# Weight tiles of the 512-column products, moved by 8 bytes within 256

## The chip, the cores and the metric

The kernel runs on one core of a Trainium2 chip. The metric is the device time of one execution in microseconds (us), as the median of several runs. Instruction durations and distances between instructions are given in nanoseconds (ns). The engines are called as in the profile: PE is TensorE's matmul, PEld its weight load, DVE VectorE, ACT ScalarE, POOL GpSimd, SP SyncE.

## The reference

One decoder layer in float32, sequence 512, model width 1024, with everything multiplied by weights that come from HBM. Cut to its products:

```
proj = h @ w_in                      # q, k, v, pool input, gate logits
y_attn = moba_attention(q, k, v) @ w_branch_attn
y_pool = multiscale_pool(p) @ w_branch_pool
mixed = sigmoid(g0) * y_attn + sigmoid(g1) * y_pool
h = layer_norm(ALPHA * h + mixed @ w_out)
a, u = split(h @ w_ffn_in)           # 2 x 2816 columns
a = causal_dwconv(a)                 # width 3
f = (gelu(a) * u) @ w_ffn_out
h = layer_norm(ALPHA * h + f)
```

## The kernel before, in words

Each float32 operand of a large product is split into two float32r tiles: hi, a rounded copy that ACT writes (line 74), and lo, the rest, which DVE writes as source minus hi (line 75). A product tile is then three matmuls that accumulate in one PSUM bank: hi with hi, hi with lo, lo with hi (`mm3`, lines 236 to 242; the v product has its own loop at line 411). Each matmul is a pair of instructions, a weight load of the 128x128 stationary operand on PEld and a matmul on PE that streams the moving operand. The load of the next pair's stationary operand runs while the present matmul streams.

Weights come in as chunks of 128 partitions by 1024 columns. `fetch` (line 128) starts the DMA into a raw tile, splits it and puts the two tiles into a ring of five slots for each of hi and lo (`slot`, line 121); a few of `w_out`'s chunks go to a pool of their own, `ext`. `weights(i)` runs `fetch` three chunks ahead. A slot is 1088 elements wide (`SLOT = D + 64`), of which 1024 are used: 4352 bytes, 17 times 256, so that all slots of the ring begin at the same place within 256 bytes.

There are two kinds of products.

- 256-column products: the moving operand is an activation of 256 columns, the stationary one is a 128x128 block of a weight tile. These are the seven-product forms of the input projection (out tiles `sai`, `sbi`, `sci`), of the gates (`sag`, `sbg`, `scg`) and of the gated MLP's first projection (`saf`, `sbf`, `scf`), in `seven`, and the first five tiles of that projection (`fi`), which run in two halves.
- 512-column products. Here the roles differ. In the pool input (`p`), the gates (`g`), the branch projections (`br`) and the rest of `fi` the weight block is stationary and the activation of 512 columns moves. In v (`v`), the output projection (`wo`) and the MLP's second projection (`foe`, `foa`, `fob`, `fod`) the activation block is stationary and 512 columns of the weight tile move. The last tile of the second projection, `fo_cut`, is cut into pieces of 256 columns, with the weight moving too.

The pools are laid out so that, without an offset, both operands of all these products begin at the same place within 256 bytes (byte 192 in this program's allocation). `slot` has an argument `near`: with it the two tiles begin `BESIDE = 2` elements, 8 bytes, behind the slot's beginning. `fetch_seven` (line 203) passes it, and `fetch` (line 151) for the first five chunks of the MLP's first projection: so the stationary operand of all 256-column products but `fo_cut` begins 8 bytes behind the moving operand's place. All 512-column products, and `fo_cut`, have both operands at the same place.

The tile framework orders each engine's instructions by a schedule and sets the semaphores; PE runs the products one behind the other in the order v, p and the first sevens, gates with attention, branch projections, the gates' sevens, output projection, MLP first projection, MLP second projection.

Of the kernel before, what the change touches and what calls it, by code (L numbers as in the profile page):

```python
# [9 lines left out]
F32R = mybir.dt.float32r  # L10
# [4 lines left out]
P = 128  # L15
S = 512
D = 1024
# [15 lines left out]
RING = 5  # L33
SLOT = D + 64
BESIDE = 2
TMP = 7
PLAIN = (3, 2)
WARM = 6
# [12 lines left out]
def layer_kernel(ctx: ExitStack, tc: tile.TileContext, xT, x, w_v, w_c, rel_bias, invcnt, w_group,  # L51
# [18 lines left out]
    def split(hi, lo, src, copy=None):  # L70
        if copy:
            copy(hi, src)
        else:
            state["hi"] = nc.scalar.activation(hi, src, AF.Copy)  # L74
        state["lo"] = nc.vector.tensor_tensor(lo, src, hi.bitcast(F32), op=ALU.subtract)  # L75
        return state["lo"]
# [30 lines left out]
    WO0 = len(chunks)  # L107
    chunks += [w_out[k * P:(k + 1) * P, :] for k in range(KT)]
    FI0 = len(chunks)
# [6 lines left out]
    FO0 = len(chunks)  # L116
# [1 line left out]
    ready = {}  # L118


    def slot(i, n, near=False):
        o = BESIDE if near else 0
        return tuple(wp.tile([P, SLOT], F32R, tag=f"w{q}", name=f"w{q}{i}", bufs=RING)[:, o:o + n]
                     for q in ("hi", "lo"))

# [2 lines left out]
    def fetch(pool=None, early=None):  # L128
        i = state["next"]
        state["next"] = i + 1  # L130
        for q, ahead in AHEAD.items():
            while coming[q]:
                key = coming[q][0]
                n, f = key
                lead_ = EARLY.get((n, f, q), ahead)
                if not homes.get((n, q)) or at[n, f, q] > i + (lead_ if q != "A" or (n, f - 1) in pair_of else 0):
                    break
                with ExitStack() as held:
                    if (n, f, q) == ("i", 1, "X"):
                        held.enter_context(tc.issue_after(state["neg"].ins))  # L140
                    if (n, f, q) in (("i", 1, "D"), ("i", 2, "A"), ("i", 2, "X"), ("i", 2, "D")):
                        held.enter_context(tc.issue_after(state["plain"].ins))
                    if (n, f, q) == ("i", 2, "X"):
                        held.enter_context(tc.issue_after(state["sum"].ins))
                    fetch_raw(coming[q].pop(0), q)
        if isinstance(chunks[i], tuple):
            ready[i] = (fetch_fo if i >= FO0 else fetch_seven)(i, *chunks[i])
            return
        raw = wp.tile([P, D], F32, tag="wraw", name=f"wraw{i}", bufs=3)
        if pool is None:  # L150
            hi, lo = slot(i, D, FI0 <= i < FI0 + RING)
        else:
            hi = pool.tile([P, D], F32R, name=f"whi{i}")
            lo = pool.tile([P, D], F32R, name=f"wlo{i}")
        parts = 2 if early else 1
        for c in range(parts):
            sl = slice(c * (D // parts), (c + 1) * (D // parts))
            (nc.scalar if early else nc.sync).dma_start(raw[:, sl], chunks[i][:, sl])
            split(hi[:, sl], lo[:, sl], raw[:, sl])
            if c == 0 and early:  # L160
                state["w0"] = raw[:, sl]
                early()
        ready[i] = (hi, lo)
# [10 lines left out]
    def fetch_raw(key, q):  # L174
        a, u = pair_of[key]
        r = raws[key, q] = homes[key[0], q](key[1])
        if q == "A":
            nc.sync.dma_start(r, a)
        elif q == "D":
            nc.sync.dma_start(r, u[:, S:])  # L180
        elif key in SUMMED:
            state["plain"] = nc.sync.dma_start(r[:, :S], u[:, :S])
        else:
            v = r.rearrange("p (a c) -> p a c", a=2)
            (pst, pn), (est, _) = u.ap
            state["plain"] = nc.sync.dma_start(
                v, bass.AP(tensor=u.tensor, offset=u.offset, ap=[[pst, pn], [0, 2], [est, S]]))
            state["acc"] = nc.gpsimd.dma_start(  # L188
                v, bass.AP(tensor=a.tensor, offset=a.offset, ap=[[pst, pn], [u.offset + S - a.offset, 2], [est, S]]),
                accum_op=ALU.add)  # L190

    def fetch_seven(i, key, q):
        n = S if q == "D" else D
        raw = raws[key, "A" if q == "Y" else q]
        if q == "X" and key in SUMMED:
            with tc.issue_after(state["Y"].ins):
                for c, o in ((slice(S, D), raws[key, "D"]), (slice(0, S), raws[key, "A"][:, :S])):
                    nc.vector.tensor_tensor(raw[:, c], raw[:, :S], o, op=ALU.add)
        if q == "Y":

            for c, o in ((slice(0, S), raws[key, "X"][:, S:]), (slice(S, D), raw[:, :S])):
                nc.vector.tensor_tensor(raw[:, c], o, raw[:, c], op=ALU.add)
        hi, lo = slot(i, n, True)
        state[q] = split(hi, lo, raw)
        return hi, lo

# [6 lines left out]
    def fetch_fo(i, name, c):  # L213
        sl = piece(c)
        n = sl.stop - sl.start
        step = {"T3": "=B11", "B11": "+B12", "T1": "+B22", "T2": "+B21", "T4": None}
        if name in step:
            raw = tw[:, sl]
        else:
            raw = wp.tile([P, D], F32, tag="wraw", name=f"wraw{i}", bufs=3)[:, :n]  # L220
            nc.sync.dma_start(raw, half(name, sl))
        hi, lo = slot(i, n)
        split(hi, lo, raw)
        then = step.get(name)
        if then and then[0] == "+":
            nc.gpsimd.dma_start(raw, half(then[1:], sl), accum_op=ALU.add)
        elif then:
            nc.sync.dma_start(raw, half(then[1:], sl))
        return hi, lo

    def weights(i):
        while state["next"] <= min(i + LEAD, state["limit"]):
            fetch()
        return ready[i]
# [97 lines left out]
    for kt in range(KT):  # L332
        xk = xr[kt // 4][:, kt % 4, :]
        if kt == 0:
            load_x(kt, xk, slice(0, 256), nc.vector.tensor_copy)
            fetch(early=lambda: load_x(kt, xk, slice(256, 512), nc.vector.tensor_copy))
        else:
            load_x(kt, xk)
            if kt % 2 == 0:
                fetch()  # L340
# [100 lines left out]
    def pool_sum(j, b, sign=1.0, eng=None):  # L441
        eng = eng or nc.gpsimd
        w = POOL_WINDOWS[j]
        pt = pb.tile([P, PAD + S], F32, tag="tmp", name=f"pt{j}", bufs=TMP)
        nc.gpsimd.memset(pt[:, :PAD], 0.0)
        state["pt"] = nc.scalar.activation(pt[:, PAD:], b, AF.Copy, scale=sign)
        cur, sh = pt, 1
        while sh < w:
            nxt = pb.tile([P, PAD + S], F32, tag="tmp", name=f"pw{j}_{sh}", bufs=TMP)
            o = 2 * sh - 1  # L450
# [251 lines left out]
    def gate_done(f, ba, u):  # L702
        if f < KT - 1:
            for br, v, scale in ((0, ba, 1.0), (1, u, -1.0)):
                nc.scalar.activation(v, v, AF.Sigmoid, scale=scale)
                nc.vector.tensor_tensor(branch[f, br], branch[f, br], v, op=ALU.mult)
            merged(f, branch[f, 0], branch[f, 1])
        else:
            for br, v, scale in ((0, ba, 1.0), (1, u, -1.0)):
                gslot[8 * br + f] = unused.pop(0)  # L710
                nc.scalar.activation(gslot[8 * br + f], v, AF.Sigmoid, scale=scale)
# [6 lines left out]
    for f in range(GSEVEN, KT):  # L718
        if f == KT - 1:
# [3 lines left out]
              lambda ba, u, f=f: gate_done(f, ba, u), first_half if f == KT - 1 else None)  # L723
# [411 lines left out]
```

## Time and profile before

| what | value |
|---|---|
| median of 3 runs | 631.38 us (631.32 to 631.77) |
| span of the profiled execution, first to last instruction | 630.0 us |
| between the span and the median of the runs | 1.4 us |
| PE busy, share of the span | 620.1 us, 98% |
| PEld / DVE / ACT / POOL busy | 552.1 / 495.0 / 346.9 / 115.3 us |
| matmuls on PE | 3904 |
| mean granted TensorE clock | 0.995 |
| moved by DMA | 105.33 MB, 167 GB/s |

For the profiled execution the profile gives the span alone; its own time is taken as the span and the 1.4 us around it. A matmul's duration in a row (389 ns for 512 columns) is its way through the pipeline; what a stream of them costs is the distance from one start to the next, called the pitch here.

### The profile page before, as it was taken

The numbers are of one execution on the slowest core, as the hardware profiler recorded it, in microseconds if no ns is written. First come the engines' busy times: TensorE is split into PE (matmuls) and PEld (weight loads), VectorE is DVE, ScalarE is ACT, GpSimd is POOL, SyncE is SP. The second block draws the span as 40 slices with busy tenths as digits, with TensorE's granted clock in tenths as the row PEclk, the third lists the DMA queues.
The fourth block names the chain that finished last, engine by engine and source line by source line (L and its number), as shares of the span: only waits on it lengthen the run. The fifth ranks groups of instructions, "written<-read, shape, count | busy, mean of one in ns | idle before, by whom it ended". The sixth has DMA issues, their size and how long they took to land.

```text
span 630.0 us, 10173 instructions
## 1 busy us (share of the span) xinstructions
PE 620.1 (98%) x3904; PEld 552.1 (88%) x3904; DVE 495.0 (79%) x751; ACT 346.9 (55%) x517; POOL 115.3 (18%) x128
## 2 busy tenths in 40 slices
PE   9999999999999999999999999999999999999994
PEld 6899998777788998889989999999998888888884
DVE  6978787776495788399767899888889649798796
ACT  6646776654634567134545665565665345555452
POOL 0133134423142101110010101101002002123302
PEclk9999999999999999999999999999999999999997
DMA  8567647522558525805096677777539946889905
GB/s 311 172 187 188 176 119 224 135 85 67 168 127 212 129 74 161 323 12 167 5 250 164 164 206 183 202 175 193 139 107 325 267 134 133 207 194 211 257 1 133
DMA packets 38912, 105.33 MB, mean 167 GB/s; under 512 B 4288, under 2 KB 4552, under 8 KB 38608
## 3 DMA queue, kind: packets, MB, share of 16 engines
q1 hardware_dynamic: 26448, 71.11, 34.1%
q0 software_dynamic: 11840, 32.53, 26.5%
q10 hardware_dynamic: 576, 1.05, 0.5%
q8 instruction: 30, 0.49, 0.3%
q14 instruction: 18, 0.15, 0.1%
HBM read 99.41 MB, written 3.17 MB: 163 GB/s over the span
## 4 chain that ended last, share of the span: by engine, by line
PE 98%; DVE 1%; DMA 1%; DVEq 0%; issue 0%
PE fi L238 5%; PE fi L241 5%; PE fi L242 5%; PE saf L238 4%; PE saf L241 4%; PE saf L242 4%; PE v L411 3%; PE br L238 2%; PE g L238 2%; PE g L242 2%; PE g L241 2%; PE wo L241 2%; PE br L241 2%; PE wo L242 2%; PE wo L238 2%; PE br L242 2%
## 5 line engine op out<-in xcount | busy, mean ns | idle before, releaser
L74 ACT ACTIVATE whi<-wraw 128x1024 fp32r<-128x1024 f32 (+1 forms) x59 | 60.2, 1027 | 44.4 <-DMA wraw<-in_w_fo 9.4
L75 DVE TENSOR_TENSOR wlo<-wraw,whi 128x1024 fp32r<-128x1024 f32 (+1 forms) x59 | 72.3, 1233 | 15.0 <-ACT whi L74 14.7
L75 DVE TENSOR_TENSOR wlo<-araw,whi 128x1024 fp32r<-128x1024 f32 x46 | 56.0, 1227 | 11.4 <-ACT whi L74 10.7
L74 ACT ACTIVATE whi<-araw 128x1024 fp32r<-128x1024 f32 x46 | 48.1, 1057 | 19.2 <-PE saf L241 4.9
L241 PE MATMUL fi<-hT_lo,whi 128*128 128x512 f32 (+1 forms) x168 | 56.3, 336 | 0.0
L242 PE MATMUL fi<-hT_hi,wlo 128*128 128x512 f32 (+1 forms) x168 | 56.3, 336 | 0.0
L238 PE MATMUL fi<-hT_hi,whi 128*128 128x512 f32 (+1 forms) x168 | 56.1, 338 | 0.0
L188 POOL DMA_DIRECT2D xraw<-in_w_fi x14 | 16.9, 1207 | 159.1 <-DMA xraw<-in_w_fi 79.4
L74 ACT ACTIVATE whi<-tw 128x1024 fp32r<-128x1024 f32 (+1 forms) x30 | 29.4, 983 | 24.1 <-PE fi L241 10.5
L75 DVE TENSOR_TENSOR wlo<-tw,whi 128x1024 fp32r<-128x1024 f32 (+1 forms) x30 | 33.3, 1126 | 7.9 <-ACT whi L74 7.8
L242 PEld LDWEIGHTS fi<-hT_hi,wlo 128*128 128x128 f32 x168 | 31.5, 188 | 3.5
L241 PEld LDWEIGHTS fi<-hT_lo,whi 128*128 128x128 f32 x168 | 31.5, 188 | 3.3
L238 PEld LDWEIGHTS fi<-hT_hi,whi 128*128 128x128 f32 x168 | 31.3, 188 | 3.4
L549 POOL TENSOR_SCALAR pp<-pp,rs 128x128 f32<-128x128 f32 (+3 forms) x32 | 25.3, 805 | 36.6 <-DVE rs L546 26.6
L238 PE MATMUL sbf<-T_hi,whi 128*128 128x256 f32 x112 | 31.2, 279 | 0.0
L241 PE MATMUL saf<-hT_lo,whi 128*128 128x256 f32 x112 | 31.2, 278 | 0.0
L238 PE MATMUL saf<-nT_hi,whi 128*128 128x256 f32 x112 | 31.2, 278 | 0.0
L238 PE MATMUL saf<-hT_hi,whi 128*128 128x256 f32 x112 | 31.1, 278 | 0.0
L242 PE MATMUL saf<-nT_hi,wlo 128*128 128x256 f32 x112 | 31.1, 278 | 0.0
L241 PE MATMUL sbf<-T_lo,whi 128*128 128x256 f32 x112 | 31.1, 278 | 0.0
L242 PE MATMUL sbf<-T_hi,wlo 128*128 128x256 f32 x112 | 31.1, 278 | 0.0
L241 PE MATMUL saf<-nT_lo,whi 128*128 128x256 f32 x112 | 31.1, 277 | 0.0
(340 smaller groups left out, 2090.5 us busy)
## 6 DMA issues: line engine op xcount, KB each, us to landing
tw<-in_w_fo POOLq DMA_DIRECT2D x20, 512.0 KB, 8.5
wraw<-in_w_fi SPq DMA_DIRECT2D x16, 512.0 KB, 3.5
araw<-in_w_fi SPq DMA_DIRECT2D x14, 512.0 KB, 4.0
xraw<-in_w_fi SPq DMA_DIRECT2D x14, 512.0 KB, 4.4
xraw<-in_w_fi POOLq DMA_DIRECT2D x14, 512.0 KB, 6.2
wraw<-in_w_c SPq DMA_DIRECT2D x10, 512.0 KB, 3.9
tw<-in_w_fo SPq DMA_DIRECT2D x10, 512.0 KB, 6.3
wraw<-in_w_fo SPq DMA_DIRECT2D x10, 512.0 KB, 7.6
```

What stands on the lines that cost most here:

```text
L74: state["hi"] = nc.scalar.activation(hi, src, AF.Copy)
L75: state["lo"] = nc.vector.tensor_tensor(lo, src, hi.bitcast(F32), op=ALU.subtract)
L188: state["acc"] = nc.gpsimd.dma_start(v, bass.AP(tensor=a.tensor, offset=a.offset, ap=[[pst, pn], [u.offset + S - a.offset, 2], [est, S]]), ...
L238: ins = nc.tensor.matmul(out_, wh, ah, start=start, stop=False, **kw)
L241: nc.tensor.matmul(out_, wh, al, start=False, stop=False, **kw)
L242: nc.tensor.matmul(out_, wl, ah, start=False, stop=stop, **kw)
L411: nc.tensor.matmul(bs[j], xs_[j][a], (wh, wl)[b], start=kt == 0 and n == 0, stop=False)
L549: nc.gpsimd.tensor_scalar(pp[:, offs[i]:offs[i] + n], pp[:, offs[i]:offs[i] + n], rs[:, i:i + 1], 1.0, op0=ALU.mult, op1=ALU.mult)
```

## The change

All split weight tiles of the ring and of `ext` now begin 8 bytes off. Where the weight is stationary (p, g, br, the rest of `fi`, and as before the sevens) the tile begins 8 bytes behind the slot's beginning. Where the weight moves (v, the output projection, the second projection with `fo_cut`) it begins 62 elements, 248 bytes, behind it, which is 8 bytes ahead of the place within 256. In either case the stationary operand then begins 8 bytes behind the moving operand's place. The tiles of `ext` become 1088 elements wide. No instruction is added, removed or reordered in the source.

```
+MOVED = 62
...
-    def slot(i, n, near=False):
-        o = BESIDE if near else 0
+    def beside(i):
+        return MOVED if i < 4 or WO0 <= i < FI0 or i >= FO0 else BESIDE
+
+    def slot(i, n):
+        o = beside(i)
         return tuple(wp.tile([P, SLOT], F32R, tag=f"w{q}", name=f"w{q}{i}", bufs=RING)[:, o:o + n]
                      for q in ("hi", "lo"))
...
-            hi, lo = slot(i, D, FI0 <= i < FI0 + RING)
+            hi, lo = slot(i, D)
         else:
-            hi = pool.tile([P, D], F32R, name=f"whi{i}")
-            lo = pool.tile([P, D], F32R, name=f"wlo{i}")
+            hi, lo = (pool.tile([P, SLOT], F32R, name=f"w{q}{i}")[:, beside(i):beside(i) + D] for q in ("hi", "lo"))
...
-        hi, lo = slot(i, n, True)
+        hi, lo = slot(i, n)
```

Chunks 0 to 3 are v's; `WO0` to `FI0` are the output projection's, from `FO0` on the second projection's.

## Rows read from the trace of the kernel before

**Rows 1.** The page: busy time of each engine, share of the span, instructions.

```profile
PE 620.1 (98%) x3904; PEld 552.1 (88%) x3904; DVE 495.0 (79%) x751; ACT 346.9 (55%) x517; POOL 115.3 (18%) x128
```

**Rows 2.** Who PE waited for: us in total, times, longest.

```profile
PE warm_ps L326 <- DVE warm L323: 1.2, 1, 1.2
```

**Rows 3.** Matmul groups by shape, whole span: count | busy us, mean ns | idle.

```profile
L238 PE MATMUL fi<-hT_hi,whi 128*128 128x512 f32 x88 | 34.3, 389 | 0.0
...
L238 PE MATMUL g<-xT_hi,whi 128*128 128x512 f32 x64 | 25.5, 399 | 0.0
L238 PE MATMUL wo<-whi,mx_hi 128*128 128x512 f32 x64 | 25.0, 390 | 0.0
...
L238 PE MATMUL foa<-whi,sd_hi 128*128 128x512 f32 x44 | 17.1, 389 | 0.0
...
L238 PE MATMUL foe<-whi,sd_hi 128*128 128x512 f32 x33 | 12.9, 390 | 0.0
...
L238 PE MATMUL br<-zT_hi,whi 128*128 128x512 f32 x32 | 12.6, 393 | 0.0
...
L238 PE MATMUL fob<-whi,sd_hi 128*128 128x512 f32 x22 | 8.6, 389 | 0.0
...
L411 PE MATMUL v<-whi,xT_hi 128*128 128x512 f32 x27 | 8.1, 413 | 0.0
...
L238 PE MATMUL p<-xT_hi,whi 128*128 128x512 f32 x16 | 6.2, 390 | 0.0
...
L238 PE MATMUL fo_cut<-whi,sd_hi 128*128 128x256 f32 x22 | 6.2, 282 | 0.0
...
L238 PE MATMUL v<-whi,xT_hi 128*128 128x512 f32 x4 | 1.6, 389 | 0.0
```

**Rows 4.** Timeline of PE, one product of the second projection: start us, us.

```profile
531.06 0.39 PE L238 MATMUL foa<-whi,sd_hi 128*128 128x512 f32 x1
...
546.02 0.39 PE L238 MATMUL fob<-whi,sd_hi 128*128 128x512 f32 x1
```

**Rows 5.** Timeline of PE, the run of 256-column pieces at the end.

```profile
616.27 0.28 PE L238 MATMUL fo_cut<-whi,sd_hi 128*128 128x256 f32 x1
...
621.07 0.28 PE L241 MATMUL fo_cut<-wlo,sd_hi 128*128 128x256 f32 x1
```

**Rows 6.** Timeline of PE, the sevens of the MLP's first projection.

```profile
340.01 0.28 PE L242 MATMUL sbf<-T_hi,wlo 128*128 128x256 f32 x1
...
470.01 0.28 PE L242 MATMUL saf<-nT_hi,wlo 128*128 128x256 f32 x1
```

**Rows 7.** Weight loads by shape, 616.2 to 621.1 us: count | busy us, mean ns.

```profile
L238 PEld LDWEIGHTS fo_cut<-whi,sd_hi 128*128 128x128 f32 x14 | 2.7, 192 | 0.0
```

**Rows 8.** Weight loads by shape, 531.1 to 546 us.

```profile
L238 PEld LDWEIGHTS foa<-whi,sd_hi 128*128 128x128 f32 x21 | 3.9, 188 | 0.8
```

**Rows 9.** Weight loads by shape, 340 to 470 us.

```profile
L238 PEld LDWEIGHTS sbf<-T_hi,whi 128*128 128x128 f32 x110 | 20.7, 188 | 0.0
```

**Rows 10.** Matmuls running at 336.43 us, by shape.

```profile
L242 PE MATMUL fi<-hT_hi,wlo 128*128 128x512 f32 x1 | 0.4, 391 | 0.0
L241 PE MATMUL fi<-hT_lo,whi 128*128 128x512 f32 x1 | 0.4, 389 | 0.0
```

**Rows 11.** Timeline of PE, three pairs between two pieces of 256 columns.

```profile
608.66 0.40 PE L238 MATMUL foe<-whi,sd_hi 128*128 128x512 f32 x1
...
609.36 0.28 PE L238 MATMUL fo_cut<-whi,sd_hi 128*128 128x256 f32 x1
```

**Rows 12.** ACT's groups by shape, 165 to 600 us.

```profile
L74 ACT ACTIVATE whi<-wraw 128x1024 fp32r<-128x1024 f32 x37 | 38.8, 1057 | 30.9 <-DMA wraw<-in_w_fo 9.0 <-DMA wraw<-in_w_fi 4.5 <-DMA wraw<-in_w_out 4.3
L74 ACT ACTIVATE whi<-araw 128x1024 fp32r<-128x1024 f32 x36 | 37.8, 1058 | 16.4 <-PE saf L241 4.9 <-PE scf L241 3.9 <-PE br L241 1.9
```

**Rows 13.** DVE by stretch: us, busy (instructions), PE clock, DMA share, GB/s.

```profile
245.30:290.60 45.30, 34.28 (x65) 1.00 0.43 156
...
516.00:606.00 90.00, 74.58 (x83) 1.00 0.76 176
```

## The prediction

> **What bounds the kernel.** I read the page first: PE is busy for 620.1 of the 630.0 us [rows 1]. Then the waits: PE waited once, 1.2 us ahead of its first matmul, and for nothing after that [rows 2]. So the end is set by the stream of weight loads and matmuls alone, and a change that only shifts where weight tiles begin can act in one way: by the pitch, the distance from one matmul's start to the next. That is read from the timeline, as first and last row of a long stretch with the count between them. Three stretches matter:
>
> - 512 columns, both operands at the same place: from 531.06 to 546.02 us lie 66 pairs (11 blocks of the contraction, two row tiles, three matmuls), 14.96 / 66 = 226.7 ns each [rows 4].
> - 256 columns, same place: 616.27 to 621.07 us, 40 pairs, 120.0 ns each [rows 5].
> - 256 columns, stationary operand 8 bytes behind: 340.01 to 470.01 us, 1125 pairs, 115.6 ns each [rows 6].
>
> At the same place the two widths differ by 106.7 ns for 256 columns, which is one column per cycle at the 2.4 GHz level; the clock rows of two stretches of 512-column work show 1.00 granted [rows 13]. So 512 columns alone are 213.3 ns, and both widths carry the same 13.3 ns on top (226.7 - 213.3, 120.0 - 106.7). With the stationary operand 8 bytes behind, only 115.6 - 106.7 = 8.9 ns are on top. What the 8 bytes are worth in 256 columns is the difference of the two, 4.4 ns a pair.
>
> **The change, part by part.** *The 512-column pairs.* Their groups count 88 (fi), 64 (g), 64 (wo), 44 (foa; fod has as many), 33 (foe), 32 (br from zT; as many from oT), 22 (fob), 27 and 4 (v) and 16 (p) for one of the three matmuls [rows 3]: 88 + 64 + 64 + 88 + 33 + 64 + 22 + 31 + 16 = 470, times three is 1410 pairs. 696 of them (p, g, br, fi) have the weight stationary, 714 (v, wo, second projection) have it moving. No row shows a 512-column stretch with the stationary operand 8 bytes behind, so the price is bounded. Below, nothing excludes that all of the 13.3 ns goes: 1410 x 13.3 = 18.8 us. Above, the dearest pitch of settled neighbours that I find is that of three pairs between two 256-column pieces, 608.66 to 609.36 us, 233 ns each [rows 11]: 6.7 ns more than now, 9.4 us in all. Between these ends I take the value of the row that differs in just this one thing at the other width: 8.9 on top instead of 13.3. The reason is that the load lies beside the beginning of the matmul it overlaps in both widths, and that at the same place the surcharge does not depend on the width; if it is one surcharge per load, the 8 bytes should cut it alike. That is 1410 x 4.4 = 6.2 us.
>
> *The last tile, fo_cut.* 22 x 3 = 66 pairs of 256 columns go from the same place to 8 bytes off [rows 3]: 66 x 4.4 = 0.3 us. The roles are reversed there (weight moving), which the 115.6 ns row does not cover; the term is small either way.
>
> *Pairs where the relation changes today.* Between 512- and 256-column products the relation of the operands jumps now and won't afterwards. One such pair is 391 ns long where its neighbour is 389 [rows 10]. There are some twenty such borders, so a few tenths of a us at most; I leave them out of the sum.
>
> *The splits.* ACT writes a hi tile in 1057 ns where it begins at the slot's beginning (`wraw` beyond the first five fi chunks) and in 1058 ns where it begins 8 bytes on (`araw`) [rows 12], so the offset costs the splitting engines nothing. Where PE gets faster, they must follow: in the second projection DVE is busy for 74.58 of 90 us, in the output projection for 34.28 of 45.3 [rows 13]. A PE that is 2% faster shortens 90 us to 88.2, still 13 us above DVE's work. Chunks are fetched three ahead, and a chunk of the second projection lasts 12 pairs, 2.7 us. If that cover were gone, each us won would come back as a wait of PE for a lo tile; nothing in the waits says it is near.
>
> *DMA and memory.* No transfer, queue entry or wait is added or moved. The three chunks in `ext` need 1536 bytes more per partition in all; that is an allocation and no instruction.
>
> **Sum.** 6.2 + 0.3 = 6.5 us off the profiled execution: a span of 623.5 us. The median lies 1.4 us above the span, so 624.9 us.
>
> **A rule against it.** The trace says that the operands' relation within 256 bytes moves the pitch by 4.4 ns. The Trainium skill's page SBUF — State Buffer, section "Who interferes with whom", gives TensorE two independent read ports, one for the moving operand and one for the weight load, and says that PE never waits on anyone. By that rule no offset could change a pitch and the sum would be 0, against the two 256-column stretches here; as a result it is the first rival.
>
> **The rivals.** *No change: the load sets the 256-column pitch, and only there.* The load rows speak for this. In the slow 256-column stretch a load lasts 192 ns [rows 7]; 8 bytes off it lasts 188 [rows 9], and that 4 ns is just about what the pitch gained. In the 512-column product the load already lasts 188 ns [rows 8] and has 227 ns to hide in. Then the offset shortens a load that sets the pace at 256 columns and is hidden at 512; the equal 13.3 ns would be an accident. Only fo_cut gains: 631.4 - 0.3 = 631.1 us. Against it: two exactly equal surcharges at two widths ask for one cause.
>
> *Slower: 512 columns are best at the same place.* The mechanism is that the moving stream, not the load, pays for the offset, over its whole width. One pair bears it out: the last 512-column matmul of fi before a seven runs beside a load that already is 8 bytes off, and is 391 ns long instead of 389 [rows 10]; it did not get shorter. If 2 ns stay with every pair, 1410 x 2 = 2.8 us are lost: 631.4 + 2.8 = 634.2 us, and up to 640.8 us at 233 ns a pair. It decides as soon as the settled pitch is above 226.7 ns plus 0.9. Against it: a single pair at a border is not a settled stretch. The 256-column pairs behind such a border take some pairs to come down to 115.6 ns as well.
>
> *One role alone gains.* If only the 696 pairs with a stationary weight win 4.4 ns, 3.1 us come off (628.3); if only the 714 with a moving one do, about the same. This lies inside the forecast's own range and has no chance of its own.
>
> **How the numbers follow.** Forecast, faster: 0.47. No change: 0.20. Slower: 0.33. A measurement of this kernel can tell about 0.2% from no change, 1.3 us or 0.9 ns a pair, so the three signs have the same chances. The forecast's own range is 616 to 630 us, from 11 ns won per pair to 1 ns. With both signs in play the range must reach into the slower case: 619 to 636 us leaves out some 0.05 below (more than 9 ns won per pair) and some 0.09 above (more than 3.3 ns lost).
>
> **What would show it.** In the profile after: the same 66 pairs of the second projection in 14.67 us (222.2 ns) for the forecast, 14.96 us for no change, 15.1 us or more for the slower case; fo_cut at about 115.6 ns, its loads at 188 ns; the same comparison in the branch projections, where the weight is stationary, tells the roles apart; no new wait on PE. The forecast is wrong if the surcharge of a 512-column pair has another cause than that of a 256-column pair, or if the settled pitch depends on something that long streams find by themselves, which the uneven pitches at borders hint at.

## The result and the profile after

The changed kernel is slower: 637.51 us median (637.2 to 638.13, four runs) against 631.54 us (631.32 to 631.77), a ratio of 1.0092 [1.0078, 1.0107]. The forecast was 624.9 us. It missed by 12.6 us, and the result lies above the range's upper end of 636 us as well. The profiled execution has a span of 636.0 us where before had 630.0, so the profile shows the 6.0 us.

The page of the kernel after, its line of busy times:

```profile
PE 626.2 (98%) x3904; PEld 552.6 (87%) x3904; DVE 495.7 (78%) x751; ACT 346.5 (54%) x517; POOL 114.6 (18%) x128
```

The waits of PE in the kernel after:

```profile
PE warm_ps L329 <- DVE warm L326: 1.2, 1, 1.2
```

PE is busy for 6.1 us longer, with as many instructions, and waits no more than before [rows 1, 2]. PE's matmuls come in the same order in both kernels. So the time lies in the pitches, as the prediction said it must. Here are first and last row of five stretches of the kernel after, from the timeline of PE (start us, us); they are the branch projections, the output projection, the 256-column sevens of the MLP's first projection, the second projection, and the pieces of `fo_cut` at the end:

```profile
171.40 0.39 PE L244 MATMUL br<-oT_lo,whi 128*128 128x512 f32 x1
...
198.62 0.39 PE L245 MATMUL br<-zT_hi,wlo 128*128 128x512 f32 x1
...
252.24 0.39 PE L244 MATMUL wo<-wlo,mx_hi 128*128 128x512 f32 x1
...
279.66 0.39 PE L244 MATMUL wo<-wlo,mx_hi 128*128 128x512 f32 x1
...
343.32 0.28 PE L241 MATMUL sbf<-T_hi,whi 128*128 128x256 f32 x1
...
469.97 0.28 PE L244 MATMUL saf<-nT_lo,whi 128*128 128x256 f32 x1
...
535.33 0.39 PE L241 MATMUL foa<-whi,sd_hi 128*128 128x512 f32 x1
...
550.62 0.39 PE L241 MATMUL fob<-whi,sd_hi 128*128 128x512 f32 x1
...
623.70 0.28 PE L241 MATMUL fo_cut<-whi,sd_hi 128*128 128x256 f32 x1
...
626.94 0.28 PE L241 MATMUL fo_cut<-whi,sd_hi 128*128 128x256 f32 x1
```

The branch and output projections of the kernel before were not among the rows shown; the same 118 pairs of each in its timeline:

```profile
170.12 0.39 PE L241 MATMUL br<-oT_lo,whi 128*128 128x512 f32 x1
...
196.87 0.39 PE L242 MATMUL br<-zT_hi,wlo 128*128 128x512 f32 x1
...
250.26 0.39 PE L241 MATMUL wo<-wlo,mx_hi 128*128 128x512 f32 x1
...
277.01 0.39 PE L241 MATMUL wo<-wlo,mx_hi 128*128 128x512 f32 x1
```

| stretch | pairs | before, ns | after, ns |
|---|---|---|---|
| branch projections, weight stationary | 118 | 26.75 us / 118 = 226.7 | 27.22 us / 118 = 230.7 |
| output projection, weight moving | 118 | 26.75 us / 118 = 226.7 | 27.42 us / 118 = 232.4 |
| second projection, weight moving | 66 | 226.7 [rows 4] | 15.29 us / 66 = 231.7 |
| sevens, not touched | 1096 | 115.6 [rows 6] | 126.65 us / 1096 = 115.6 |
| `fo_cut`, weight moving | 27 | 120.0 [rows 5] | 3.24 us / 27 = 120.0 |

These 512-column stretches have become slower, by 4.0 ns a pair where the weight is stationary and by 5.0 to 5.7 ns where it moves. What wasn't touched stayed, and the settled run of `fo_cut` did not react at all. At these pitches 696 x 4.0 + 714 x about 5.2 is 6.5 us, against 6.0 measured. Added up over both timelines, every 512-column stage takes longer: those with a stationary weight 2.5 us in all, the output and second projections 3.0, and v 0.6, which moves by as much in runs that leave it alone. The short stretches between borders lose a little less than the long ones.

The weight loads by shape (count | busy us, mean ns | idle us), first in the same stretch of the second projection, 535.4 to 550.6 us, then in `fo_cut`, 623.7 to 626.9 us, both of the kernel after:

```profile
L244 PEld LDWEIGHTS foa<-wlo,sd_hi 128*128 128x128 f32 x22 | 4.2, 189 | 1.0
...
L241 PEld LDWEIGHTS fo_cut<-whi,sd_hi 128*128 128x128 f32 x10 | 1.9, 191 | 0.0
```

The load in the second projection lasts 189 ns where it lasted 188 before, and PEld has idle time ahead of it as before [rows 8], and the pitch grew all the same. The duration of a load therefore does not tell the pitch of the pairs.

### The profile page after: what moved, and what is told of

Same layout as the page of the kernel before. It is cut to its first block, busy times and chain, and to the rows that moved or that the text cites. A ratio compares the mean times of both kernels' runs of the same rounds, so it can differ in the third digit from the quotient of the medians.

```text
span 636.0 us, 10173 instructions
## 1 busy us (share of the span) xinstructions
PE 626.2 (98%) x3904; PEld 552.6 (87%) x3904; DVE 495.7 (78%) x751; ACT 346.5 (54%) x517; POOL 114.6 (18%) x128
## 2 busy tenths in 40 slices
DMA packets 38912, 105.33 MB, mean 166 GB/s; under 512 B 4288, under 2 KB 4552, under 8 KB 38608
## 4 chain that ended last, share of the span: by engine, by line
PE 98%; DVE 1%; DVEq 0%; issue 0%
PE fi L245 5%; PE fi L244 5%; PE fi L241 5%; PE saf L241 4%; PE saf L244 4%; PE saf L245 4%; PE v L414 3%; PE br L241 2%; PE wo L245 2%; PE wo L241 2%; PE g L241 2%; PE wo L244 2%; PE g L244 2%; PE br L245 2%; PE g L245 2%; PE br L244 2%
```

## The experiments

In the kernels named pairs, and in *enter*, the whole layer is left out: they run nothing but groups of 48 (or 60) load-and-matmul pairs on fixed tiles, so their times are those of the pairs alone. All other kernels compute the layer.

### One role each

*stat_only* moves only the 696 pairs with a stationary weight:

```
     def beside(i):
-        return MOVED if i < 4 or WO0 <= i < FI0 or i >= FO0 else BESIDE
+        return 0 if i < 4 or WO0 <= i < FI0 or i >= FO0 else BESIDE
```

> Only the 696 512-column pairs whose weight is stationary (p, g, br, the rest of fi) get the 8 bytes; v, the output and the second projection stand as before. Theory A (any pair of 512 columns whose operands are 8 bytes apart loses its even pitch of 226.7 ns and runs at about 230.6 ns, whichever operand is the weight): 696 x 3.9 = 2.7 us slower, br pitch 230.6, wo and foa pitch back at 226.7. Rival B (the loss comes from the moving operand, which begins 8 bytes off its 16-byte place when the weight moves): no change in time, br at 226.7. Rival C (something else than the pitch, such as the allocation): the time moves with no change of pitch.

Measured: 634.45 us against 632.21, ratio 1.0039 [1.0026, 1.0052]. Its timeline of PE, branch projections and second projection:

```profile
170.27 0.39 PE L244 MATMUL br<-oT_lo,whi 128*128 128x512 f32 x1
...
197.49 0.39 PE L245 MATMUL br<-zT_hi,wlo 128*128 128x512 f32 x1
...
532.86 0.39 PE L241 MATMUL foa<-whi,sd_hi 128*128 128x512 f32 x1
...
547.82 0.39 PE L241 MATMUL fob<-whi,sd_hi 128*128 128x512 f32 x1
```

27.22 / 118 = 230.7 ns where the tile was moved, 14.96 / 66 = 226.7 ns where it wasn't. The loss is 2.2 us where theory A had 2.7; rival B, no loss with a stationary weight, fell.

*mov_only* moves only the 714 pairs with a moving weight, and `fo_cut`:

```
     def beside(i):
-        return MOVED if i < 4 or WO0 <= i < FI0 or i >= FO0 else BESIDE
+        if isinstance(chunks[i], tuple) and i < FO0 or FI0 <= i < FI0 + RING:
+            return BESIDE
+        return MOVED if i < 4 or WO0 <= i < FI0 or i >= FO0 else 0
```

> Only the 714 pairs whose weight moves (v, wo, second projection) and fo_cut get the 8 bytes. Theory A: 714 x 4.7 = 3.4 us slower (the changed kernel's wo ran at 232.6 ns, the second projection at 231.6), br back at 226.7 ns; the two halves add up to the 6 us. Rival B: all of the 6 us.

Measured: 636.1 us against 632.21, ratio 1.0061 [1.0046, 1.0076]. Its timeline of PE in the second projection:

```profile
532.55 0.39 PE L243 MATMUL foa<-whi,sd_hi 128*128 128x512 f32 x1
...
547.85 0.39 PE L243 MATMUL fob<-whi,sd_hi 128*128 128x512 f32 x1
```

15.30 / 66 = 231.8 ns here, while its branch projections stay at 226.7. The halves lose 0.39 and 0.61%, together 1.00%, against 0.92% for the whole; the 3.9 us here compare with 3.4 in theory A. So both roles lose, each by its own pitch, and nothing passes from one to the other.

### The other direction

*reversed* puts the stationary operand 8 bytes ahead of the moving one in the 512-column products and `fo_cut`, and leaves the other 256-column products as they were:

```
     def beside(i):
-        return MOVED if i < 4 or WO0 <= i < FI0 or i >= FO0 else BESIDE
+        if isinstance(chunks[i], tuple) and i < FO0 or FI0 <= i < FI0 + RING:
+            return BESIDE
+        return BESIDE if i < 4 or WO0 <= i < FI0 or i >= FO0 else MOVED
```

> As the changed kernel, but in all 512-column pairs and fo_cut the stationary operand begins 8 bytes ahead of the moving one instead of behind it. Theory A as it stands has no direction: as slow as the changed kernel, about 637.5 us, pitch 230 to 232. Rival D (direction decides: a load that runs ahead of the stream collides with it, one that runs behind doesn't): faster than before, up to 1410 x 4.4 = 6 us.

Measured: 640.75 us against 632.21, ratio 1.0133 [1.0116, 1.015]. Its timeline of PE in the branch projections:

```profile
172.65 0.40 PE L246 MATMUL br<-oT_lo,whi 128*128 128x512 f32 x1
...
200.19 0.40 PE L247 MATMUL br<-zT_hi,wlo 128*128 128x512 f32 x1
```

27.54 / 118 = 233.4 ns, and 232.8 in the second projection. Ahead or behind, both lose; the direction changes only how much, and rival D fell.

### The pairs alone

*pairs* runs 48 pairs for each of 11 widths with both operands at the same place. Then it moves the stationary operand, and then the moving one, in steps of 8 bytes through 256, at 512 and at 256 columns. The core of it:

```
def run(name, n, so, mo):
    b = ps.tile([P, 512], F32, tag="ps", name=name)
    for i in range(PAIRS):    # PAIRS = 48
        k, q = divmod(i, 3)
        s = sta[q == 2][:, so + k % 8 * P:so + k % 8 * P + P]
        m = mov[q == 1][:, mo + k % 4 * 512:mo + k % 4 * 512 + n]
        tc.keep_in_program_order(nc.tensor.matmul(b[:, :n], s, m, start=i == 0, stop=i == PAIRS - 1))
    ...
```

> No layer at all: 48 pairs of weight load and matmul for each of 139 settings, nothing else running. Both operands at the same place with 128 to 512 columns; then the stationary operand at 0, 8, ... 248 bytes behind it with 512 and 256 columns; then the moving operand so. Theory A: 512 columns at the same place 226.7 ns, at 8 bytes either way about 230; 256 columns 120.0 at the same place and 115.6 with the stationary operand 8 bytes behind. If one surcharge per load is right, each width at the same place costs its columns at 2.4 GHz and 13.3 ns (272 columns 126.7, 288 columns 133.3); if pairs fall into step with something of a 13.3 ns period, 272 columns cost 133.3 as 288 do. Rival E (other engines' traffic makes the difference in the layer): flat over the offsets here.

The start of each group in its timeline of PE, first by width, then by the place of the stationary operand (`a` same place, `b` 8 bytes behind, `c` 16):

```profile
41.12 0.29 PE L40 MATMUL width<-movhi,stahi 128*128 128x288 f32 x1
...
47.44 0.31 PE L40 MATMUL width<-movhi,stahi 128*128 128x320 f32 x1
...
62.80 0.36 PE L40 MATMUL width<-movhi,stahi 128*128 128x448 f32 x1
...
72.72 0.38 PE L40 MATMUL width<-movhi,stahi 128*128 128x480 f32 x1
...
104.75 0.39 PE L40 MATMUL stat_wide_a<-movhi,stahi 128*128 128x512 f32 x1
...
115.63 0.40 PE L40 MATMUL stat_wide_b<-movhi,stahi 128*128 128x512 f32 x1
...
126.71 0.39 PE L40 MATMUL stat_wide_c<-movhi,stahi 128*128 128x512 f32 x1
...
461.02 0.28 PE L40 MATMUL stat_narrow_a<-movhi,stahi 128*128 128x256 f32 x1
...
466.78 0.28 PE L40 MATMUL stat_narrow_b<-movhi,stahi 128*128 128x256 f32 x1
...
472.34 0.28 PE L40 MATMUL stat_narrow_c<-movhi,stahi 128*128 128x256 f32 x1
```

From start to next start are 48 pairs. At 512 columns 10.88 / 48 = 226.7 ns at the same place and 11.08 / 48 = 230.8 ns 8 bytes on; at 256 columns 5.76 / 48 = 120.0 and 5.56 / 48 = 115.8. These are the pitches of the layer in all four cases, with DVE, ACT and POOL idle and about 1 GB/s on the DMA queues. So they belong to PE's own stream; no neighbour is needed.

The widths show what the prediction's step could not know. The mean granted clock of this run is 0.998. Less one column per cycle of the 2.4 GHz level, the same place carries 6.32 us / 48 - 120.0 = 11.7 ns at 288 columns and 9.92 us / 48 - 186.7 = 20.0 ns at 448, beside the 13.3 at 256 and 512. At 320 and 384 columns it is 13.3 ns again, at 272 it is 12.0, at 480 and 496 16.7. So the surcharge is not one for all widths, though four of the nine from 256 up share the 13.3 ns; no run shows why. At 192 columns the last 24 pairs still take 112.6 ns each, 32.6 above the columns.

Over the 32 places of the stationary operand, 512 columns have, over the last 24 pairs of each group (the settled pitch from here on), 226.7 ns at 0 and 120 bytes and 228.3 to 234.3 at the other 30. For the moving operand it is 226.7 at 0 and 228.9 to 236.7 elsewhere. At 256 columns the order is another: 113.3 ns at 64, 88 and 168 bytes, 115.6 at 8 bytes, up to 120.1 elsewhere. With the moving operand 248 bytes behind, which is 8 bytes ahead within 256, it is 120.0 at 256 columns, as in `fo_cut`, and 232.8 at 512, where the layer has 231.7 and 232.4. In both of these ways the stationary operand lies 8 bytes behind the moving one, and the tiles are the same; what differs is where the two lie together. So that the two roles of the weight differ in the layer needs no cause but the place.

### Is it the relation alone, and is it the load?

*pairs2* repeats this with other offsets, with both operands moved together, and with loads of 64 and 32 columns in place of 128:

```
def run(name, n, so, mo, cols=P, pairs=PAIRS):
    ...
        s = sta[q == 2][:, so + k % 6 * P:so + k % 6 * P + cols]
...
for j, o in enumerate((64, 128, 192, 256, 66, 130, 194, 258)):   # elements of 4 bytes
    run(f"period_{w_}_{LETTERS[j]}", n, o, 0)
for j, o in enumerate((2, 4, 16, 32, 48)):
    run(f"both_{w_}_{LETTERS[j]}", n, o, o)
for j, o in enumerate((0, 2, 4, 8, 16)):
    run(f"half_{w_}_{LETTERS[j]}", n, o, 0, 64)
```

> No layer: 48 pairs for each setting again. (1) The stationary operand 0 to 28 bytes behind in steps of 4. (2) 256, 512, 768, 1024 bytes behind and 8 more than each: if the relation within 256 bytes is all that counts, as at 0 and at 8 bytes (226.7 and 230.6 at 512 columns, 120.0 and 115.6 at 256). (3) Both operands moved by 8, 16, 64, 128, 192 bytes together: 226.7 and 120.0 each if only the relation counts. (4) A stationary operand of 64 and of 32 columns, so that the load reads half and a quarter: if what is on top of the columns' time comes from the load's reading beside the stream, it falls with the load's length (from 13.3 ns at the same place to about 6.7 and 3.3 at 512 columns); if it is a fixed cost of a pair, it stays. (5) 0, 8, 64, 120 bytes and back in reverse order: the same pitches whatever came before, if a stream settles by itself.

Starts of some groups in its timeline of PE, the last two at 256 columns:

```profile
200.99 0.40 PE L40 MATMUL both_wide_a<-movhi,stahi 128*128 128x512 f32 x1
...
212.12 0.39 PE L40 MATMUL both_wide_b<-movhi,stahi 128*128 128x512 f32 x1
...
223.16 0.39 PE L40 MATMUL both_wide_c<-movhi,stahi 128*128 128x512 f32 x1
...
234.05 0.39 PE L40 MATMUL both_wide_d<-movhi,stahi 128*128 128x512 f32 x1
...
255.90 0.39 PE L40 MATMUL half_wide_a<-movhi,stahi 128*64 128x512 f32 x1
...
266.94 0.39 PE L40 MATMUL half_wide_b<-movhi,stahi 128*64 128x512 f32 x1
...
575.73 0.28 PE L40 MATMUL half_narrow_a<-movhi,stahi 128*64 128x256 f32 x1
...
581.20 0.28 PE L40 MATMUL half_narrow_b<-movhi,stahi 128*64 128x256 f32 x1
```

With the stationary operand 256, 512, 768 or 1024 bytes behind, the settled pitch is 226.7 ns, like 0; 8 bytes more bring 230.5 to 230.8 each time, so at these two places the pattern of the stationary operand repeats every 256 bytes (for the moving one this was not run). But both operands moved together by 8 bytes have 11.13 / 48 = 231.9 ns, by 16 bytes 230.0, and by 64 bytes 226.9: the relation is not all, the place of both counts too. And at 512 columns a load of half the columns makes the pair no faster but slower, 11.04 / 48 = 230.0 ns at the same place; a quarter has 231.7. At 256 columns it is the other way: half has 5.47 / 48 = 114.0 ns (113.3 settled), a quarter 117.8, where the whole load has 120.0. A surcharge that the load pays by its length, once per pair, is ruled out by the 512 columns and by the quarter being dearer than the half.

Two further parts of this run: steps of 4 bytes up to 28 gave 230.0 to 235.0 ns at 512 columns and 115.6 to 133.3 at 256; and four places were run in one order and back, where each had its pitch again but 64 bytes at 256 columns, which had 117.8 ns forth and 113.3 back.

### Places that were best for 256 columns in the pairs

Can the layer have the 113.3 ns? *near64*, *near88* and *near168* leave the 512-column products at the same place, as before, and move the 256-column weights from 8 to 64, 88 and 168 bytes:

```
-BESIDE = 2
+BESIDE = 16     # near64; 22 in near88, 42 in near168
```

> The kernel before with one number changed: the stationary operand of its 2172 256-column pairs (the sevens and the first five fi tiles) begins 64 instead of 8 bytes behind the moving one; 512-column pairs stay at the same place. Theory A2 (the settled pitch of a stream of pairs is a property of its width and the operands' relation within 256 bytes, so the test of pairs alone gives the layer's): 113.3 ns a pair instead of 115.6, 2172 x 2.2 = 4.8 us faster, ratio 0.992; 512-column pairs unchanged at 226.7. Rival F (in the layer the other engines' writes and the blocks' order set the pitch, and 8 bytes were found there): pitch unlike the test's, no gain or a loss.

> The same with 88 bytes, the second place at which the test of pairs alone settled at 113.3 ns, though 80 and 96 bytes, 8 to either side, gave 118.6 and 117.2. Theory A2: 113.3 ns a pair, 4.8 us faster as with 64 bytes. Rival F: another pitch. A smooth dependence on the distance (rival G): about 116 ns or more, as its neighbours.

> The kernel before with the stationary operand of the 2172 256-column pairs 168 bytes behind the moving one, the third place at which the test of pairs settled at 113.3 ns. Theory A3 (relation and width leave a stream one or a few settled cycles, and which of them it falls into depends on how it starts): between 113.3 and 118 ns, and not the same in each stage; if 113.3 in all stages, 4.8 us faster than before. Theory A2 (the pair test's number is the only one): 113.3 everywhere.

Measured: near64 636.57 us against 631.9, ratio 1.0072 [1.006, 1.0085]; near88 628.89 against 631.9, 0.9958 [0.9944, 0.9971]; near168 638.77 against 631.88, 1.0107 [1.009, 1.0124]. The same pitch in the pairs, three answers in the layer: the sevens of near64 run at 117.8 ns, those of near88 at 113.3, those of near168 at 120.0, above the 113.3 to 118 ns that were expected there. The timeline of PE in near64, sevens of the MLP:

```profile
341.74 0.28 PE L238 MATMUL sbf<-T_hi,whi 128*128 128x256 f32 x1
...
470.00 0.28 PE L238 MATMUL saf<-nT_hi,whi 128*128 128x256 f32 x1
```

128.26 us for 1089 pairs, 117.8 ns. And in near168 a stretch of `fi`'s halves and then the sevens:

```profile
312.51 0.28 PE L242 MATMUL fi<-hT_hi,wlo 128*128 128x256 f32 x1
...
319.08 0.28 PE L242 MATMUL fi<-hT_hi,wlo 128*128 128x256 f32 x1
...
342.43 0.28 PE L238 MATMUL sbf<-T_hi,whi 128*128 128x256 f32 x1
...
469.99 0.28 PE L242 MATMUL saf<-hT_hi,wlo 128*128 128x256 f32 x1
```

6.57 us / 58 = 113.3 ns, then 127.56 us / 1063 = 120.0: one kernel, one width, one relation, two pitches, each held over a long stretch. Its first sevens have both on the same products and tiles, 120.0 ns over the 86 pairs from 38.90 us and 113.3 over the 105 pairs from 53.66 us. near88 is the mirror of it: its sevens run at 113.3 ns over 1115 pairs, and a late stretch of `fi`'s halves at 116.7. The expectations that took the pitch of the pairs as a property of the place alone fell.

### Does the start decide?

*pairs3* first asks whether it is the 4-byte operands, with bfloat16 pairs at five places, and looks for any place at which 512 columns are below 226.7 ns. The core of the first part:

```
def run_half(name, n, so):
    ...
        a, z = so + i % 12 * P, i % 3 * 512
        tc.keep_in_program_order(nc.tensor.matmul(b[:, :n], half_s[:, a:a + P], half_m[:, z:z + n], ...))
...
for n in (512, 256):
    for o in (0, 4, 8, 32, 60):
        run_half("sixteen_wide" if n == 512 else "sixteen_narrow", n, o)
```

> No layer: 48 pairs a setting. (1) bfloat16 operands, half the bytes per column, with 512 and 256 columns: if what lies on top of the columns' time comes from reading 4-byte columns beside a 4-byte load, it shrinks to a few ns and no longer depends on the offset; if it is a fixed cost of a pair, 13 ns and more stay. (2) The odd 4-byte offsets from 36 to 252 bytes at 512 and 256 columns, and an offset of only hi or only lo, of either operand, at 512: theory A expects the same place to stay the best at 512 columns or to be met by few others (226.7), most at 230 to 235; a pitch clearly below 226.7 would be a better kernel.

Its timeline of PE, where the first of 240 wide and the first of 240 narrow bfloat16 pairs start:

```profile
23.61 0.82 PE L52 MATMUL sixteen_wide<-halfm,halfs 128*128 128x512 bf16 x3
...
75.43 0.38 PE L52 MATMUL sixteen_narrow<-halfm,halfs 128*128 128x256 bf16 x2
```

51.82 us / 240 = 215.9 ns over all five places, 2.6 ns above the columns alone, and 109.2 ns for the narrow ones; none of the five places differs from another. So the dependence on the place was seen with the 4-byte operands alone. Of 68 further settings of the 512-column pairs (odd multiples of 4 bytes, or only the hi or only the lo tile of one operand moved) none was below 226.7 ns; seven equalled it, most lay at 230 to 236. At 256 columns 52, 76 and 204 bytes had 113.3 ns as well.

*enter* runs each place from eight different starts: 11 pairs of 512 columns, one pair of a width that differs from start to start, then 48 pairs of the width in question. The pitch is that of the last 24.

```
def run(name, n, so, enter):
    ...
        o = 0 if i < 12 else so
        m_ = 512 if i < 11 else enter if i == 11 else n
        ...
```

> No layer: each setting's 48 pairs come behind 11 pairs of 512 columns at the same place and one pair of 160, 208, 256, ... or 512 columns that shifts their start against it, eight starts for each of four offsets at 512 columns (0, 8, 60, 120 bytes) and of eight at 256 (0, 8, 52, 64, 76, 88, 168, 204). Theory A3 (a stream settles into one of a few cycles of its relation, by its start): 0 bytes at 512 columns settles at 226.7 and 8 bytes at 230.6 from all eight starts, 8 bytes at 256 columns at 115.6 from all; 64, 88 and 168 bytes at 256 columns split between 113.3 and 116 to 120. An offset that reaches 113.3 from all eight would be better than 88 bytes in the layer. Theory A2 (one pitch for each relation): no split anywhere; the layer's split would then come from the other engines.

| columns, stationary operand behind by | pitch from eight starts, ns |
|---|---|
| 512, 0 bytes | 226.7 in all |
| 512, 8 bytes | 230.5 to 230.8 in all |
| 512, 60 bytes | 230.0 in six, 233.3 in two |
| 512, 120 bytes | 226.7 in all |
| 256, 0 bytes | 120.0 in all (120.1 in one) |
| 256, 8 bytes | 115.5 to 115.6 in all |
| 256, 52 bytes | 113.3 in seven, 120.0 in one |
| 256, 64 bytes | 113.3 in three, 117.8 in five |
| 256, 76 bytes | 113.3 in all |
| 256, 88 bytes | 113.3 in five, 116.7 in three |
| 256, 168 bytes | 113.3 in three, 120.0 in five |
| 256, 204 bytes | 113.3 in three, 120 to 123.3 in five |

Two of the eight starts at 64 bytes in its timeline of PE, 34 pairs each:

```profile
665.81 0.28 PE L42 MATMUL narrow<-movlo,stahi 128*128 128x256 f32 x1
...
669.81 0.28 PE L42 MATMUL narrow<-movhi,stalo 128*128 128x256 f32 x1
...
674.04 0.28 PE L42 MATMUL narrow<-movlo,stahi 128*128 128x256 f32 x1
...
677.89 0.28 PE L42 MATMUL narrow<-movhi,stalo 128*128 128x256 f32 x1
```

4.00 / 34 = 117.6 ns and 3.85 / 34 = 113.2 ns (117.8 and 113.3 over the last 24), on the same tiles, with nothing but the width of one earlier pair changed. So in the pairs the start decides at some places. That it does so in the layer is not shown by a run of its own, but the second values are those that the layer showed: 117.8 in near64, 116.7 in near88, 120.0 in near168. At 0, 8, 76 and (512) 120 bytes all eight starts ended alike.

*near76* takes the place at which all eight starts gave the best pitch, with 512 columns left at the same place:

```
-BESIDE = 2
+BESIDE = 19
```

> The kernel before with the stationary operand of its 2172 256-column pairs 76 bytes behind the moving one, the one offset that reached 113.3 ns from all eight starts of the test. Theory A3: 113.3 ns in every stage, the first sevens and the fi halves too, which 88 and 168 bytes did not give: 2172 x 2.2 = 4.8 us faster than before, ratio 0.992. Rival F (the layer has starts that the test has not): split pitches again, and less gain than with 88 bytes or none.

Measured: 627.89 us (627.76 to 628.47) against 631.44, ratio 0.9945 [0.9932, 0.9959]: faster than both kernels. Its timeline of PE, the sevens of the MLP:

```profile
338.60 0.28 PE L238 MATMUL sbf<-T_hi,whi 128*128 128x256 f32 x1
...
464.97 0.28 PE L242 MATMUL sbf<-T_hi,wlo 128*128 128x256 f32 x1
```

126.37 us / 1115 = 113.3 ns, and 113.3 over 58 pairs of `fi`'s halves too: both kinds of stretch over which near88 and near168 had split. The gain is 3.5 us where 4.8 was expected. Added up over the timelines of the profiled executions, the 256-column pairs take 4.6 us less, so the pitch came as expected; the rest of PE's stream takes 0.5 us more there, and the span falls by 4.0, from 630.0 to 626.0 us. Where that half microsecond comes from was not shown.

## Why the prediction was wrong

**What bounds the kernel** was right: the order of PE's stream, its waits and the untouched pitches stayed, and the whole difference lies in the pitch of the 512-column pairs.

**The step that failed** is the price of those pairs: "at the same place the surcharge does not depend on the width; if it is one surcharge per load, the 8 bytes should cut it alike". Two rows with 13.3 ns were taken for a law. The widths between them show 11.7 to 20.0 ns, a shorter load does not shrink the surcharge at 512 columns, and 8 bytes that save 4.4 ns at 256 columns cost 4.0 (weight stationary) or 5.0 to 5.7 ns (weight moving) at 512. The term was forecast at -6.2 us and came out at +6.0. The other reason, that the load lies beside the beginning of the matmul in both widths, did not fit its own rows either: a load's row lasts 188 ns [rows 8, 9], which leaves part of a 227 ns pitch uncovered at 512 columns but is longer than the whole 115.6 ns at 256.

**The bound that was nearer.** The upper bound for a 512-column pair was 233 ns, read between two 256-column pieces of this same kernel [rows 11]. The settled pitches after, 230.7 to 232.4 ns, lie close to it, and far from 222.2. That was luck: the row is three pairs at the same place just behind another width, not a settled stretch 8 bytes off. Still, of two nearest rows, the one of the same width was the better guide than the one with the same offset.

**`fo_cut`** was forecast at -0.3 us and its settled run moved by nothing. The prediction noted that its roles are reversed and took the value of the other role all the same. The pairs show that the two ways to be 8 bytes apart are not alike: 256 columns have 115.6 ns with the stationary operand 8 bytes behind and 120.0 ns with the moving one 8 bytes ahead.

**The rivals.** "Slower: 512 columns are best at the same place" had the right sign and place; its price of 2 ns from a single border pair [rows 10] was too small by half or more. Its mechanism, that the moving stream pays for the offset over its whole width, does not fit: the same offset saves 4.4 ns at 256 columns. "No change" fell with the 512-column pitches, though its warning that the equal 13.3 ns might not stand for one cause was right. "One role alone gains" fell with stat_only and mov_only.

**The rule against it.** By the Trainium skill's page SBUF — State Buffer, section "Who interferes with whom", PE has two independent read ports and never waits on anyone, from which the prediction worked out that no offset would matter. The pairs, with every other engine idle, have 226.7 to 236.7 ns at 512 columns by nothing but the place of one operand. The measurement decides: the pitch depends on the place of PE's own two operands.

**The parts costed at nothing** held: PE has no new wait, the DMA queues carry the same 105.33 MB, and the borders between widths, with all that happens in short stretches, are at most the 0.5 us by which the sum at settled pitches and the measurement differ.

**What would make it wrong** was named in the last sentence: that long streams find their settled pitch by themselves. The runs show such settled pitches. Their dependence on the start was seen at other places, not at 0 and 8 bytes, where all eight starts ended alike; so what made the forecast miss is the pitch that 8 bytes have at 512 columns, and not the start.

**What stays open.** Why a stream of 4-byte pairs settles into these cycles is not settled. The runs show that it depends on the width, on the relation of the operands within 256 bytes, on their common place, on the length of the load and at some places on the start, that it needs no other engine, and that it did not appear with bfloat16 at five places. Whether the load and the matmul get in each other's way somewhere, and where, was not shown.

## What to carry to other kernels

Price a change of operand placement in the width and the role in which it will run, with a stream of such pairs alone: at 512 columns it gave the layer's pitches to within 1.2 ns, while a saving carried over from another width had the wrong sign. At 256 columns a stream from one start was not enough: at 64 and 168 bytes it was 4.5 and 6.7 ns below the layer. So run the stream from several different starts and take the place that settles alike from all of them: 76 bytes at 256 columns made the layer 0.55% faster, while 64 bytes, whose best pitch is the same, made it 0.72% slower. Leave alone what already has the best pitch of a scan, as 512 columns had at the same place.

## What the runs showed of the hardware

A stream of 4-byte pairs settles into a short cycle and keeps it: 227, 226, 227 ns at the same place and 512 columns, 234, 230, 231, 229, 229 ns at 8 bytes, 120 ns each at 256 columns and the same place. Two such cycles can exist for the same tiles and the same instructions (113.3 and 120.0 ns at 168 bytes in *enter* and in the first sevens of near168), and in near168 a stretch of over a thousand pairs did not leave the one that it fell into. A load of 32 columns in place of 128 makes the 512-column pairs slower, 231.7 against 226.7 ns, and the 256-column pairs faster, 117.8 against 120.0. bfloat16 pairs show none of it: 215.9 and 109.2 ns at five places, 2.6 and 2.5 ns above one column per cycle; the best 4-byte pairs seen carry 6.7 ns at 256 columns and 13.3 at 512.
